# First eight column blocks as whole float32 products, and one pair of places for all operands, in a two-layer hybrid mixer on one Trainium2 core

## The chip, the core and the metric

The kernel runs on one core of a Trainium2 chip. The core has a matmul engine (PE, with a weight-load row PEld beside it), a vector engine (DVE), a scalar engine (ACT), GpSimd (POOL) and SyncE (SP), which here only issues loads. The metric is the device time of one execution in microseconds (us); lower is better.

## What is computed

Two layers over 256 tokens of width 2048. Each layer modulates its normed input by a projection of a condition vector `c`, runs two mixers side by side (a gated linear attention and an RWKV-7 recurrence), projects out, and runs a squared-ReLU feed-forward part:

```python
cond = silu(c)
for i in range(2):
    mod = cond @ w_ada[i] + b_ada[i]                 # 6 x 2048 numbers
    sh1, sc1, gt1, sh2, sc2, gt2 = split(mod, 6)
    h = rmsnorm(x, g_pre_mix[i]) * (1.0 + sc1) + sh1
    z = h @ w_in[i]
    y = concat([gla(z), rwkv7(z)]) @ w_out[i]
    x = x + gt1 * rmsnorm(y, g_post_mix[i])
    h = rmsnorm(x, g_pre_ffn[i]) * (1.0 + sc2) + sh2
    y = square(relu(h @ w_ff1[i])) @ w_ff2[i]
    x = x + gt2 * rmsnorm(y, g_post_ffn[i])
```

Everything is float32.

## The kernel before

**Tiling.** Activations lie transposed: width in 16 slices (index k) of 128 partitions, 256 tokens along the free axis. A *block* is 128 columns of a weight matrix times all 16 slices. Float32 weights are split (`split`): ScalarE copies half a weight tile, 128x1024, to a rounded `hi`, VectorE subtracts to get `lo`. The activations are split the same way into `hh` and `hl`. A block is then 16 times three products: hi·hh, hi·hl, lo·hh, 48 matmuls of 128x256 in all.

**The first stage** is `first_norm`. The norm of layer 0 needs the modulation, so for each k it runs two modulation jobs (`ada_job`, shift row k and scale row 16 + k). A job loads 1 MB of `w_ada` and reduces it against `cond` (which stands in all 128 partitions) in one VectorE instruction, `raw<-raw,cond`; small instructions (`ada_done`) add the bias and form the scale. Then `norm_block` makes slice k: VectorE multiplies x by the norm's `rstd` into `f` (tile name `f512`, two buffers), ScalarE applies scale and shift in place and copies to `hh`, VectorE subtracts to `hl`. Since every block needs all 16 slices, the kernel keeps eight blocks of `w_in` open in eight PSUM banks and grows all eight by slice k as soon as it is there (`grow`): the half megabyte of weights `w8[k]` is split and 8 x 3 matmuls run. Thirty-two modulation loads share six buffers, the sixteen `w8` loads three.

**After it** the first eight blocks are taken out of PSUM (`lerp`, tiles `th`, `gl`, `al`, `o`), and the other blocks of `w_in` run, mixed with the chains of the two mixers. The other modulation jobs are spread over later stages as a background stream.

**Places.** The operands `hh` and `hl` of a stage lie in two buffers of 16 x 256 floats with 64 floats of room; `HOME` gives, for each of six operands, at how many floats from the 256-byte-aligned start `hh` and `hl` begin. Operand 0 is the input of layer 0's mixers, 1 its out projection, 2 its feed-forward input, 3 to 5 the same in layer 1. The squared hidden activations (`hid`) have one pair, 12 and 284, which is 12 and 28 past a multiple of 64.

**Order.** Each engine runs its instructions strictly in the order in which the built program has them. That order is made by a scheduler when the kernel is built, not by the order of the source lines; priorities (`high_priority`) shift it.

Of the kernel before, what the change touches and what calls it, by code (L numbers as in the profile page):

```python
# [8 lines left out]
F32 = mybir.dt.float32  # L9
# [3 lines left out]
ALU = mybir.AluOpType  # L13
# [28 lines left out]
for _name, _n in (("g1", 16), ("gg1", 16), ("g2", 16), ("gg2", 16), ("omu", 29), ("h_k_k", 8), ("h_w0", 8),  # L42
                  ("h_a0", 8), ("h_v0", 8), ("h_k_a", 8), ("c_k_a", 8), ("h_norm_w", 8), ("h_gn_w", 8)):
    _DER[_name] = (NDER, _n)
    NDER += _n
# [50 lines left out]
HOME = ((24, 8), (12, 28), (4, 36), (8, 40), (36, 4), (60, 28))  # L96
# [72 lines left out]
class Kernel:  # L169
# [16 lines left out]
    def setup(self, pool):  # L186
        nc, a, c = self.nc, self.a, self.const

        c1, sg = (pool.tile([P, 512], F32, name=n, bufs=1) for n in ("c1", "sg"))
        nc.gpsimd.memset(c1, 0.0)  # L190
        nc.sync.dma_start(out=c1[0:P:32], in_=a["c"])
        cs = c.tile([P, 4, P], F32, name="cs")
        nc.sync.dma_start(out=cs, in_=a["cst"])
        self.ident, self.bd, self.ones, self.center = (cs[:, n] for n in range(4))
# [4 lines left out]
        self.mod = c.tile([P, 2, 96], F32, name="mod")  # L199
        self.der = c.tile([P, 2, NDER], F32, name="der")  # L200

        self.tanh(sg, c1, scale=0.5)
        nc.vector.scalar_tensor_tensor(c1, sg, 1.0, c1, ALU.add, ALU.mult)
        self.cond = c.tile([P, D], F32, name="cond")
# [7 lines left out]
        self.eps = c.tile([P, 4], F32, name="eps")  # L212
        for n, e in enumerate((1e-6, GN_EPS, KK_SCALE * 1e-24, -KK_SCALE * 1e-24)):
            nc.vector.memset(self.eps[:, n:n + 1], e)
        self.rstd = c.tile([P, T], F32, name="rstd")
        self.shift = c.tile([P, NF], F32, name="shift")
        self.shs = c.tile([P, KT, 2, 2], F32R, name="shs")
        self.vfirst = self.dram.tile([8, P, T], F32, name="vfirst")
        self.spill = self.dram.tile([2, 8, P, 5, T], F32, name="spill")
        self.vmix = self.dram.tile([8, P, T], F32, name="vmix")  # L220

    def constants(self):
        nc = self.nc
        for i in range(2):
# [22 lines left out]

    def tanh(self, out, in_, bias=0.0, scale=1.0, more=()):

        ins = self.nc.scalar.activation(out, in_, AF.Tanh, bias=bias, scale=scale)  # L250
        for o, x, b, c in more:
            ins = self.nc.scalar.activation(o, x, AF.Tanh, bias=b, scale=c)
        with self.tc.issue_after(ins.ins):
            self.nc.scalar.preload_act_table_set(BASE_SET)


    def ada_job(self, i, j, single=None):
# [3 lines left out]
        nc.sync.dma_start(out=raw, in_=self.a["ada"][i, j])  # L261
        nc.vector.tensor_tensor_reduce(  # L262
            out=raw, in0=raw, in1=self.cond, op0=ALU.mult, op1=ALU.add, scale=1.0, scalar=0.0,
            accum_out=self.mod[:, i, j:j + 1])
# [5 lines left out]
    def ada_done(self, i, j0, j1):  # L270

        nc = self.nc
        seg, k = j0 // 16, slice(j0 % 16, j0 % 16 + j1 - j0)
        m = self.mod[:, i, j0:j1]
        nc.vector.tensor_tensor(m, m, self.col(i, "b_ada")[:, j0:j1], op=ALU.add)

        name, g = (None, ("g1", "g_pre_mix"), ("gg1", "g_post_mix"),
                   None, ("g2", "g_pre_ffn"), ("gg2", "g_post_ffn"))[seg] or (None, None)
        if name is None:
            return  # L280
        d = self.dcol(i, name)[:, k]
        if seg in (1, 4):
            nc.vector.scalar_tensor_tensor(d, m, 1.0, self.col(i, g)[:, k], ALU.add, ALU.mult)
        else:
            nc.vector.tensor_tensor(d, m, self.col(i, g)[:, k], op=ALU.mult)
        nc.vector.tensor_scalar(d, d, -0.5 / D, None, ALU.mult)
# [88 lines left out]
    def first_norm(self, pool, rstd):  # L375

        nc = self.nc
# [5 lines left out]
        for k in range(KT):  # L383
            self.ada_job(0, k, pool)
            self.ada_job(0, 16 + k, pool)
            self.norm_block(pool, 0, rstd, 0, k, 1)
# [4 lines left out]
            hi, lo = self.split(raw, P)  # L391
            self.grow(hi, lo, self.hh[:, k], self.hl[:, k], k)

    def boundary(self, pool, i, y, acc, which, ni, src, out=None):
# [27 lines left out]
        for k in range(0, KT, 2):  # L422
            us = []
            self.update(i, y, r, which, k)
            for q in range(2):
# [3 lines left out]
                nc.scalar.activation(u[0][:, :T], self.x[:, k + q], AF.Copy, scale=self.dcol(ni, g, k + q))  # L429
                nc.vector.scalar_tensor_tensor(u[1][:, :T], self.x[:, k + q], self.dcol(ni, g, k + q),  # L430
# [22 lines left out]
    def norm_block(self, pool, i, rstd, which, k, n):  # L453
        nc = self.nc
        g, s0 = ("g1", 0) if which == 0 else ("g2", 48)
        t = pool.tile([P, n, T], F32, name="f512")
        nc.vector.tensor_tensor(t, self.x[:, k:k + n], rstd.unsqueeze(1).broadcast_to([P, n, T]), op=ALU.mult)
        for q in range(n):
            nc.scalar.activation(t[:, q], t[:, q], AF.Identity, scale=self.dcol(i, g, k + q),
                                 bias=self.mod[:, i, s0 + k + q:s0 + k + q + 1])  # L460
        hh, hl = self.hh[:, k:k + n], self.hl[:, k:k + n]
        nc.scalar.copy(hh, t)
        nc.vector.tensor_tensor(hl, t, hh.bitcast(F32), op=ALU.subtract)

# [578 lines left out]
    def layer(self, i):  # L1043
        nc, a = self.nc, self.a
        with ExitStack() as ctx:
# [12 lines left out]
            for m in range(KT):  # L1058
                ps = self.block(a["wout"][i, m], lambda k: oh[:, k], lambda k: ol[:, k], OUT_ORDER)
                nc.scalar.activation(y[:, m], ps, AF.Copy, scale=self.dcol(i, "gg1", m))  # L1060
# [13 lines left out]
            for c in range(4):  # L1074
# [19 lines left out]
                for m in range(KT):  # L1094
# [5 lines left out]
                    if c == 3:  # L1100
                        acc = self.accumulate(pool, acc, y[:, m], m == KT - 1)
                        nc.scalar.activation(y[:, m], y[:, m], AF.Copy, scale=self.dcol(i, "gg2", m))
# [88 lines left out]
def _pack(x):  # L1191
# [4 lines left out]
    a["c"] = f["c"].reshape(4, 512)  # L1196
# [60 lines left out]
```

## Time and profile before

| | us |
|---|---|
| median of 3 runs | 2750.57 (2744.34 to 2753.77) |
| the profiled execution | 2763.49 |
| its span, first to last instruction | 2761.7 |
| busy: PE / PEld | 2624.6 (95%) / 2516.8 (91%) |
| busy: DVE / ACT / POOL | 1994.7 (72%) / 1417.7 (51%) / 67.7 (2%) |
| chain that ended last | PE 76%, DVE 10%, DMA 8%, ACT 3%, issue 2% |

A line number such as L306 is a line of the kernel before. Busy times are sums of durations; matmuls are pipelined, so the time from one matmul's start to the next one's is read instead of the duration. The row PEclk gives the granted clock of PE as a share of 2.4 GHz; it has two levels, 2.4 and 1.2 GHz. The span is one execution; the runs' median lies 12.9 us under the profiled execution's own time.

### The profile page before, as it was taken

To read this page: it belongs to the slowest core of one execution; us is meant where nothing else is said; L and a number is where in the kernel's file an instruction comes from. 1 tells how busy PE (TensorE), PEld (TensorE's weight loads), DVE (VectorE), ACT (ScalarE), POOL (GpSimd) and SP (SyncE) were. 2 spreads that over 40 slices of the span, in tenths; PEclk is the share of its full clock that TensorE was granted. 3 is DMA by queue.
4 is the path that set the end of the run, shared out by engine and by line. 5 is a ranking of instruction groups with operands and counts; after the bars stand their busy time and mean duration, and the time that the engine had idled before them with its cause. 6 is when DMAs were issued, how large, how long until landed. Compare 5 with 4: busy or idle time off the path is not lost.

```text
span 2761.7 us, 55614 instructions
## 1 busy us (share of the span) xinstructions
PE 2624.6 (95%) x23388; PEld 2516.8 (91%) x23388; DVE 1994.7 (72%) x2961; ACT 1417.7 (51%) x2357; POOL 67.7 (2%) x201
## 2 busy tenths in 40 slices
PE   4688999998999999999999999999989999999997
PEld 4688888888999999999989889888989999999997
DVE  8997886678876777777777698666786565565655
ACT  3377644454744534434568866445474443443453
POOL 0000000010000000000001000000000000000000
PEclk8799999999999999999999999999999999999999
DMA  9775576667677877877846547654846666666653
GB/s 402 314 271 187 178 282 238 214 248 274 221 287 285 298 289 277 297 291 281 292 181 224 184 163 254 237 174 163 330 164 216 222 219 214 216 220 220 215 185 120
DMA packets 104082, 659.20 MB, mean 239 GB/s; under 512 B 11540, under 2 KB 20884, under 8 KB 32408
## 3 DMA queue, kind: packets, MB, share of 16 engines
q1 hardware_dynamic: 87848, 618.19, 62.4%
q10 hardware_dynamic: 15984, 37.46, 3.7%
q8 instruction: 183, 3.00, 0.4%
q14 instruction: 67, 0.55, 0.1%
HBM read 638.83 MB, written 16.78 MB: 237 GB/s over the span
## 4 chain that ended last, share of the span: by engine, by line
PE 76%; DVE 10%; DMA 8%; ACT 3%; issue 2%; ACTq 0%; POOL 0%; DVEq 0%; SPq 0%
PE pm L317 13%; PE pm L319 13%; PE pm L318 12%; PE px L319 7%; PE px L317 7%; PE px L318 7%; DMA raw<-in_ada_dram 4%; DVE raw L262 3%; DVE lo L306 3%; PE p L523 1%; DMA raw<-in_ff_dram 1%; ACT hi L305 1%; DMA raw<-in_wout_dram 1%; PE px L470 1%; PE pm L1012 1%
## 5 line engine op out<-in xcount | busy, mean ns | idle before, releaser
L306 DVE TENSOR_TENSOR lo<-raw,hi 128x1024 fp32r<-128x1024 f32 (+1 forms) x792 | 957.4, 1215 | 494.6 <-ACT hi L305 489.6
L305 ACT CAST hi<-raw 128x1024 fp32r<-128x1024 f32 (+1 forms) x792 | 818.7, 1041 | 736.6 <-PE pm L318 305.9
L317 PE MATMUL pm<-hh,hi 128*128 128x256 f32 x2624 | 758.3, 289 | 5.0 <-ACT hi L305 2.7
L319 PE MATMUL pm<-hh,lo 128*128 128x256 f32 x2624 | 745.4, 284 | 5.8 <-DVE lo L306 5.6
L318 PE MATMUL pm<-hl,hi 128*128 128x256 f32 x2624 | 741.3, 283 | 0.0
L317 PEld LDWEIGHTS pm<-hh,hi 128*128 128x128 f32 x2624 | 497.3, 190 | 15.8 <-ACT hi L305 3.3
L319 PEld LDWEIGHTS pm<-hh,lo 128*128 128x128 f32 x2624 | 497.5, 190 | 10.9 <-DVE lo L306 7.3
L318 PEld LDWEIGHTS pm<-hl,hi 128*128 128x128 f32 x2624 | 497.4, 190 | 4.5 <-issue 1.6
L262 DVE CUSTOM_DVE_ANT_0 raw<-raw,cond 128x2048 f32<-128x2048 f32 x192 | 439.2, 2288 | 76.3 <-DMA raw<-in_ada_dram 75.8
L317 PE MATMUL px<-hid,hi 128*128 128x256 f32 x1024 | 287.0, 280 | 0.5 <-ACT hid L1090 0.5
L319 PE MATMUL pm<-hid,lo 128*128 128x256 f32 x1024 | 287.4, 281 | 0.0
L319 PE MATMUL px<-hid,lo 128*128 128x256 f32 x1024 | 287.4, 281 | 0.0
L317 PE MATMUL pm<-hid,hi 128*128 128x256 f32 x1024 | 286.9, 280 | 0.0
L318 PE MATMUL px<-hid,hi 128*128 128x256 f32 x1024 | 285.2, 279 | 0.4 <-DVE hid L1091 0.4
L318 PE MATMUL pm<-hid,hi 128*128 128x256 f32 x1024 | 284.7, 278 | 0.0
L319 PE MATMUL px<-hh,lo 128*128 128x256 f32 x896 | 251.3, 280 | 0.0
L317 PE MATMUL px<-hh,hi 128*128 128x256 f32 x896 | 251.2, 280 | 0.0
L318 PE MATMUL px<-hl,hi 128*128 128x256 f32 x896 | 249.8, 279 | 0.0
L318 PEld LDWEIGHTS px<-hid,hi 128*128 128x128 f32 x1024 | 192.2, 188 | 1.0 <-DVE hid L1091 0.8
L317 PEld LDWEIGHTS px<-hid,hi 128*128 128x128 f32 x1024 | 192.4, 188 | 0.7 <-ACT hid L1090 0.7
L319 PEld LDWEIGHTS px<-hid,lo 128*128 128x128 f32 x1024 | 192.8, 188 | 0.0
L319 PEld LDWEIGHTS pm<-hid,lo 128*128 128x128 f32 x1024 | 192.8, 188 | 0.0
(333 smaller groups left out, 4168.2 us busy)
## 6 DMA issues: line engine op xcount, KB each, us to landing
raw<-in_ff_dram SPq DMA_DIRECT2D x242, 1024.0 KB, 5.0
raw<-in_ada_dram SPq DMA_DIRECT2D x192, 1024.0 KB, 6.3
raw<-in_win_dram SPq DMA_DIRECT2D x90, 1024.0 KB, 5.2
raw<-in_wout_dram SPq DMA_DIRECT2D x32, 1024.0 KB, 5.6
raw<-in_ff1s_dram SPq DMA_DIRECT2D x16, 896.0 KB, 4.7
spill<-pk ACTq DMA_DIRECT2D x16, 640.0 KB, 4.7
pk<-spill ACTq DMA_DIRECT2D x16, 640.0 KB, 5.3
raw<-in_w_dram SPq DMA_DIRECT2D x16, 512.0 KB, 10.4
```

Source lines behind the costliest of these rows:

```text
L262: nc.vector.tensor_tensor_reduce(out=raw, in0=raw, in1=self.cond, op0=ALU.mult, op1=ALU.add, scale=1.0, scalar=0.0, accum_out=self.mod[:, ...
L305: self.nc.scalar.copy(hi, half)
L306: self.nc.vector.tensor_tensor(lo, half, hi.bitcast(F32), op=ALU.subtract)
L317: nc.tensor.matmul(ps, hi[:, n % 8], xh(k), start=n == 0, stop=False)
L318: nc.tensor.matmul(ps, hi[:, n % 8], xl(k), start=False, stop=False)
L319: nc.tensor.matmul(ps, lo[:, n % 8], xh(k), start=False, stop=n == KT - 1)
L470: self.nc.tensor.matmul(ps, self.ones, sq[:, q], start=k + q == 0, stop=k + q == KT - 1)
L523: self.nc.tensor.matmul(v[:, h, n + c], l[hs, cs], r[hs, cs], start=True, stop=True)
L1012: nc.tensor.matmul(vps[c], hh[:, kk, cs], hi[:, kq], start=kk == 0, stop=False)
```

## The change

- The first eight blocks are no longer split. `first_norm` multiplies the float32 tile `w8[k]` with the float32 tile `f` (returned by `norm_block`), one matmul for each block and slice; 384 matmuls of split operands become 128 of whole float32, and 16 `hi` copies on ScalarE and 16 `lo` subtractions on VectorE go. `hh` and `hl` are still made, for the later blocks.
- `ada_done` goes. Two tables, `factor` and `start`, are made once for each layer (`ada_tables`), and a job multiplies by its factor within its reduction; shift rows take `start` in there too, the others get one addition. Scales are read from `mod` (`mcol`), no longer from `der`.
- `c` is broadcast to all partitions by its load (1 MB written). The sigmoid then runs on the full 128x2048 in two halves; the four matmuls and four copies that spread `cond` go. The loads of x and of the constants change queues: x goes from ScalarE's queue to SP's, ahead of the modulation loads.
- All six operands lie at 12 and 28.

```diff
-HOME = ((24, 8), (12, 28), (4, 36), (8, 40), (36, 4), (60, 28))
+HOME = ((12, 28),) * 6
@@ setup
-        nc.sync.dma_start(out=c1[0:P:32], in_=a["c"])
+        nc.sync.dma_start(out=self.cond, in_=a["c"].broadcast_to([P, D]))
         for k in range(0, KT, 4):
-            nc.scalar.dma_start(out=self.x[:, k:k + 4], in_=a["xT"][:, k:k + 4])
+            nc.sync.dma_start(out=self.x[:, k:k + 4], in_=a["xT"][:, k:k + 4])
-        for n in range(0, D, 512):
-            ps = self.psm.tile([P, 512], F32, name="pm")
-            r = slice(n // 16, n // 16 + 1)
-            nc.tensor.matmul(ps, self.ones[r], c1[r], start=True, stop=True)
-            nc.scalar.activation(self.cond[:, n:n + 512], ps, AF.Copy, scale=0.5)
+            for h in halves:
+                nc.vector.scalar_tensor_tensor(self.cond[:, h], sg[:, h], 1.0, self.cond[:, h], ALU.add, ALU.mult)
+            self.ada_tables(0)
@@ ada_job
         nc.vector.tensor_tensor_reduce(
-            out=raw, in0=raw, in1=self.cond, op0=ALU.mult, op1=ALU.add, scale=1.0, scalar=0.0,
-            accum_out=self.mod[:, i, j:j + 1])
-        if single:
-            self.ada_done(i, j, j + 1)
-        elif j % 16 == 15:
-            self.ada_done(i, j - 15, j + 1)
+            out=raw, in0=raw, in1=self.cond, op0=ALU.mult, op1=ALU.add, scale=self.factor[:, i, j:j + 1],
+            scalar=self.start[:, i, j:j + 1] if small else 0.0, accum_out=self.mod[:, i, j:j + 1])
+        if not small and (single or j % 16 == 15):
+            js = slice(j if single else j - 15, j + 1)
+            nc.vector.tensor_tensor(self.mod[:, i, js], self.mod[:, i, js], self.start[:, i, js], op=ALU.add)
@@ first_norm
-            self.norm_block(pool, 0, rstd, 0, k, 1)
+            h = self.norm_block(pool, 0, rstd, 0, k, 1)
@@
-            hi, lo = self.split(raw, P)
-            self.grow(hi, lo, self.hh[:, k], self.hl[:, k], k)
+            w = raw.rearrange("p (n c) -> p n c", c=P)
+            for n, (ps, _, _) in enumerate(self.first):
+                nc.tensor.matmul(ps, w[:, n], h[:, 0], start=k == 0, stop=k == KT - 1)
```

The change also moves instructions. On VectorE, one k step late in the first stage stood so before (`raw` are modulation tiles, `f512` the normed slice before the split, ISA the reduction and the read of its sum; a name in brackets is the engine whose work is waited for):

```order
L262 ISA raw_743,mod_97<-raw_743,cond_102 128x2048 [waits DMAHW7_49]
L262 ISA mod_97 128x1
L275 TENSOR_TENSOR mod_97<-mod_97,par_91 128x1 [waits DVE_49]
L262 ISA raw_747,mod_97<-raw_747,cond_102 128x2048 [waits DMAHW0_49]
L262 ISA mod_97 128x1
L275 TENSOR_TENSOR mod_97<-mod_97,par_91 128x1 [waits DVE_49]
L283 SCALAR_TENSOR_TENSOR der_98<-mod_97,par_91 128x1 [waits DVE_49]
L286 TENSOR_SCALAR der_98<-der_98 128x1 [waits DVE_49]
L306 TENSOR_TENSOR lo_761<-raw8_758,hi_760 128x1024 [waits DMAHW1_49,PE_49,Activation_49]
L463 TENSOR_TENSOR hl_150<-f512_753,hh_149 128x256 [waits Activation_49]
L457 TENSOR_TENSOR f512_865<-x_84,rs_142 128x256 [waits DVE_49]
```

Between the scale (L286), which ScalarE waits for, and `hl`, which waits for ScalarE, stands the 128x1024 subtraction. On VectorE after the change, two k steps early in the first stage:

```order
L284 ISA raw_202,mod_101<-raw_202,cond_86,start_103,factor_102 128x2048 [waits DMAHW6_49]
L462 TENSOR_TENSOR f512_231<-x_84,rs_142 128x256 [waits DVE_49,PE_49]
L284 ISA raw_205,mod_101<-raw_205,cond_86,factor_102 128x2048 [waits DMAHW7_49]
L289 TENSOR_TENSOR mod_101<-mod_101,start_103 128x1 [waits DVE_49]
L468 TENSOR_TENSOR hl_150<-f512_209,hh_149 128x256 [waits Activation_49]
L284 ISA raw_224,mod_101<-raw_224,cond_86,start_103,factor_102 128x2048 [waits DMAHW1_49]
L284 ISA raw_227,mod_101<-raw_227,cond_86,factor_102 128x2048 [waits DMAHW2_49]
L462 TENSOR_TENSOR f512_253<-x_84,rs_142 128x256 [waits DMAHW5_49,DVE_49,PE_49]
L289 TENSOR_TENSOR mod_101<-mod_101,start_103 128x1 [waits DVE_49]
L468 TENSOR_TENSOR hl_150<-f512_231,hh_149 128x256 [waits Activation_49]
```

(The reads of the sums are left out.) `hl` now stands directly behind the addition that releases ScalarE, and `f`, whose buffer is read by the matmuls of two slices earlier, waits for PE; it stands alternately between the two reductions and behind both. At the end of the first stage VectorE has after the change (`lo` here is of the first block after the stage, `th` the first block taken out of PSUM):

```order
L468 TENSOR_TENSOR hl_150<-f512_473,hh_149 128x256 [waits Activation_49]
L309 TENSOR_TENSOR lo_595<-raw_592,hi_594 128x1024 [waits DMAHW5_49,Activation_49]
L309 TENSOR_TENSOR lo_599<-raw_592,hi_598 128x1024 [waits Activation_49]
L284 ISA raw_518,mod_101<-raw_518,cond_86,start_103,factor_102 128x2048 [waits DMAHW6_49]
L284 ISA raw_521,mod_101<-raw_521,cond_86,factor_102 128x2048 [waits DMAHW7_49]
L289 TENSOR_TENSOR mod_101<-mod_101,start_103 128x1 [waits DVE_49]
L468 TENSOR_TENSOR hl_150<-f512_525,hh_149 128x256 [waits Activation_49]
L284 ISA raw_715,mod_101<-raw_715,cond_86,factor_102 128x2048 [waits DMAHW1_49]
L309 TENSOR_TENSOR lo_721<-raw_718,hi_720 128x1024 [waits DMAHW2_49,Activation_49]
L514 SCALAR_TENSOR_TENSOR th_568<-pm_152,par_93,th_568 128x255 [waits DMAHW4_49,DMAHW0_49,Activation_49]
```

Before, the first two of these `lo` stood behind the last `hl`, and the third reduction and the third `lo` behind `th`. After the first stage the scheduler places many instructions of layer 0's mixers in another order; the feed-forward parts keep theirs.

## Rows read from the trace of the kernel before

**Rows 1.** Stretches: us; busy (count) of PE, PEld, DVE, ACT, POOL; PEclk, DMA, GB/s.

```profile
20.00:64.00 44.00, 24.43 (x144) 23.19 (x144) 44.00 (x77) 12.31 (x19) 0.00 (x0) 0.88 1.02 418
64.00:129.00 65.00, 40.36 (x222) 38.14 (x223) 63.19 (x102) 18.60 (x29) 0.12 (x1) 0.76 0.86 344
```

**Rows 2.** Timeline of one k step: start, duration, engine, line, operation, count.

```profile
114.82 0.42 DVE L457 TENSOR_TENSOR f<-x,rs 128x256 f32<-128x256 f32 x1
...
115.16 2.28 DVE L262 CUSTOM_DVE_ANT_0 raw<-raw,cond 128x2048 f32<-128x2048 f32 x1
...
117.57 2.29 DVE L262 CUSTOM_DVE_ANT_0 raw<-raw,cond 128x2048 f32<-128x2048 f32 x1
...
119.90 0.16 DVE L275 TENSOR_TENSOR mod<-mod,par 128x1 f32<-128x1 f32 x1
...
120.28 0.15 DVE L286 TENSOR_SCALAR der<-der 128x1 f32<-128x1 f32 x1
120.39 1.22 DVE L306 TENSOR_TENSOR lo<-raw,hi 128x1024 fp32r<-128x1024 f32 x1
120.47 0.60 ACT L459 ACTIVATE f<-f,mod,der 128x256 f32<-128x256 f32 x1 [5.19 <-DVE der L286]
...
121.54 0.42 DVE L463 TENSOR_TENSOR hl<-f,hh 128x256 fp32r<-128x256 f32 x1
...
121.89 2.28 DVE L262 CUSTOM_DVE_ANT_0 raw<-raw,cond 128x2048 f32<-128x2048 f32 x1
```

**Rows 3.** Timeline: first reduction with what precedes it; second and sixteenth `hl`.

```profile
13.71 1.05 ACT L1136 ACTIVATE sq<-x 128x1024 f32<-128x1024 f32 x1
...
16.06 0.69 DVE L1139 TENSOR_TENSOR acc<-acc 128x512 f32<-128x512 f32 x1
...
18.86 2.28 DVE L262 CUSTOM_DVE_ANT_0 raw<-raw,cond 128x2048 f32<-128x2048 f32 x1
...
33.27 0.42 DVE L463 TENSOR_TENSOR hl<-f,hh 128x256 fp32r<-128x256 f32 x1
...
128.26 0.42 DVE L463 TENSOR_TENSOR hl<-f,hh 128x256 fp32r<-128x256 f32 x1
```

**Rows 4.** Timeline behind the first stage: split, first blocks' exit, next block's first matmul.

```profile
130.23 2.36 DVE L306 TENSOR_TENSOR lo<-raw,hi 128x1024 fp32r<-128x1024 f32 x2 [1.54 <-ACT hi L305]
...
132.51 0.48 DVE L508 SCALAR_TENSOR_TENSOR th<-pm,par,th 128x255 f32<-128x255 f32 x1
...
133.03 0.38 PE L317 MATMUL pm<-hh,hi 128*128 128x256 f32 x1 [0.33 <-DVE th L508]
```

**Rows 5.** Timeline, float32 matmuls, two records each: at 1.2 GHz, at 2.4 GHz.

```profile
16.80 2.07 PE L347 MATMUL px<-acc,cs 128*128 128x256 f32 x4 [0.86 <-DVE acc L1139]
...
579.24 1.03 PE L803 MATMUL px<-gl,wsmB 128*128 128x256 f32 x4
```

**Rows 6.** One line's instructions: ns least, median, most; first and last start.

```profile
L347 PE MATMUL px<-acc,cs x12: 377/378/793, 16.8 to 2744.8; 128*128 128x256 f32 x12
```

**Rows 7.** Timeline of split matmuls in one k step, 1.2 GHz.

```profile
123.53 0.41 PE L373 MATMUL px<-hh,lo 128*128 128x256 f32 x1
123.74 0.41 PE L371 MATMUL px<-hh,hi 128*128 128x256 f32 x1
```

**Rows 8.** Timeline, first matmuls of blocks 15 blocks apart: layer 1, then layer 0.

```profile
2203.55 0.28 PE L317 MATMUL px<-hh,hi 128*128 128x256 f32 x1
...
2288.34 0.28 PE L317 MATMUL pm<-hh,hi 128*128 128x256 f32 x1
...
2299.64 0.28 PE L317 MATMUL pm<-hid,hi 128*128 128x256 f32 x1
...
2383.91 0.28 PE L317 MATMUL px<-hh,hi 128*128 128x256 f32 x1
...
1050.08 0.28 PE L317 MATMUL px<-hh,hi 128*128 128x256 f32 x1
...
1133.29 0.28 PE L317 MATMUL pm<-hh,hi 128*128 128x256 f32 x1
```

More of the change, by code (lines that the diff above doesn't have):

```diff
@@ L41 @@
 NDER = 0
-for _name, _n in (("g1", 16), ("gg1", 16), ("g2", 16), ("gg2", 16), ("omu", 29), ("h_k_k", 8), ("h_w0", 8),
+for _name, _n in (("omu", 29), ("h_k_k", 8), ("h_w0", 8),
                   ("h_a0", 8), ("h_v0", 8), ("h_k_a", 8), ("c_k_a", 8), ("h_norm_w", 8), ("h_gn_w", 8)):
@@ L187, in setup @@
         nc, a, c = self.nc, self.a, self.const
-        c1, sg = (pool.tile([P, 512], F32, name=n, bufs=1) for n in ("c1", "sg"))
-        nc.gpsimd.memset(c1, 0.0)
-        nc.sync.dma_start(out=c1[0:P:32], in_=a["c"])
-        cs = c.tile([P, 4, P], F32, name="cs")
-        nc.sync.dma_start(out=cs, in_=a["cst"])
-        self.ident, self.bd, self.ones, self.center = (cs[:, n] for n in range(4))
+        sg = pool.tile([P, D], F32, name="sg", bufs=1)
+        self.cond = c.tile([P, D], F32, name="cond")
+        self.eps = c.tile([P, 4], F32, name="eps")
+        for n, e in enumerate((1e-6, GN_EPS, KK_SCALE * 1e-24, -KK_SCALE * 1e-24)):
+            nc.vector.memset(self.eps[:, n:n + 1], e)
+        nc.sync.dma_start(out=self.cond, in_=a["c"].broadcast_to([P, D]))
         self.par = c.tile([P, 2, NPAR], F32, name="par")
@@ L197, in setup @@
         for k in range(0, KT, 4):
-            nc.scalar.dma_start(out=self.x[:, k:k + 4], in_=a["xT"][:, k:k + 4])
-        self.mod = c.tile([P, 2, 96], F32, name="mod")
-        self.der = c.tile([P, 2, NDER], F32, name="der")
-        self.tanh(sg, c1, scale=0.5)
-        nc.vector.scalar_tensor_tensor(c1, sg, 1.0, c1, ALU.add, ALU.mult)
-        self.cond = c.tile([P, D], F32, name="cond")
-        for n in range(0, D, 512):
-            ps = self.psm.tile([P, 512], F32, name="pm")
-            r = slice(n // 16, n // 16 + 1)
-            nc.tensor.matmul(ps, self.ones[r], c1[r], start=True, stop=True)
-            nc.scalar.activation(self.cond[:, n:n + 512], ps, AF.Copy, scale=0.5)
+            nc.sync.dma_start(out=self.x[:, k:k + 4], in_=a["xT"][:, k:k + 4])
+        cs = c.tile([P, 4, P], F32, name="cs")
+        nc.scalar.dma_start(out=cs, in_=a["cst"])
+        self.ident, self.bd, self.ones, self.center = (cs[:, n] for n in range(4))
+        self.mod, self.factor, self.start = (c.tile([P, 2, 96], F32, name=n) for n in ("mod", "factor", "start"))
+        self.der = c.tile([P, 2, NDER], F32, name="der")
+        with self.tc.high_priority(1000):
+            early = pool.tile([P, 1], F32, name="early", bufs=1)
+            ins = nc.scalar.activation(early, self.eps[:, 0:1], AF.Tanh)
+            with self.tc.issue_after(ins.ins):
+                halves = [slice(n, n + D // 2) for n in (0, D // 2)]
+                self.tanh(sg[:, halves[0]], self.cond[:, halves[0]], scale=0.5,
+                          more=[(sg[:, halves[1]], self.cond[:, halves[1]], 0.0, 0.5)])
+            for h in halves:
+                nc.vector.scalar_tensor_tensor(self.cond[:, h], sg[:, h], 1.0, self.cond[:, h], ALU.add, ALU.mult)
+            self.ada_tables(0)
         self.xres = self.dram.tile([P, KT, T], F32, name="xres")
-        self.eps = c.tile([P, 4], F32, name="eps")
-        for n, e in enumerate((1e-6, GN_EPS, KK_SCALE * 1e-24, -KK_SCALE * 1e-24)):
-            nc.vector.memset(self.eps[:, n:n + 1], e)
         self.rstd = c.tile([P, T], F32, name="rstd")
@@ L223, in constants @@
         nc = self.nc
+        self.ada_tables(1)
         for i in range(2):
@@ L246, in dcol, with mcol @@
         return self.der[:, i, at + k:at + k + 1]
+    def mcol(self, i, name, k):
+        j = 16 * ("s1", "g1", "gg1", "s2", "g2", "gg2").index(name) + k
+        return self.mod[:, i, j:j + 1]
     def tanh(self, out, in_, bias=0.0, scale=1.0, more=()):
@@ L254, in tanh, with ada_tables @@
             self.nc.scalar.preload_act_table_set(BASE_SET)
+    def ada_tables(self, i):
+        nc = self.nc
+        f, s, b = self.factor[:, i], self.start[:, i], self.col(i, "b_ada")
+        nc.vector.memset(f, 0.5)
+        for seg, g in ((1, "g_pre_mix"), (2, "g_post_mix"), (4, "g_pre_ffn"), (5, "g_post_ffn")):
+            nc.vector.tensor_scalar(f[:, 16 * seg:16 * seg + 16], self.col(i, g), -0.25 / D, None, ALU.mult)
+        nc.vector.scalar_tensor_tensor(s, b, 2.0, f, ALU.mult, ALU.mult)
+        for seg in (1, 4):
+            q = slice(16 * seg, 16 * seg + 16)
+            nc.vector.scalar_tensor_tensor(s[:, q], f[:, q], 2.0, s[:, q], ALU.mult, ALU.add)
     def ada_job(self, i, j, single=None):
@@ L454, in norm_block @@
         nc = self.nc
-        g, s0 = ("g1", 0) if which == 0 else ("g2", 48)
+        g, s = ("g1", "s1") if which == 0 else ("g2", "s2")
         t = pool.tile([P, n, T], F32, name="f512")
```

31 lines of the change are left out of this document (9 added, 22 removed).

## The prediction

> **What bounds the kernel now.** I read the busy time by stretches first. Over most of the span PE is full and VectorE is not; the exception is the first stage, up to 129 us, where PE is busy little more than half the time and VectorE nearly all of it (44.00 of 44, then 63.19 of 65) [rows 1]. Loads stand close behind: 418 GB/s with all DMA engines busy in the earlier stretch, 344 in the later [rows 1]. So the first stage ends when VectorE is through with its 16 steps, and the change is aimed there. The timeline of one step shows its length: its first reduction starts at 115.16, that of the next at 121.89, 6.73 us, and the `f` multiply, which this step happens to lack, adds 0.34: 7.1 [rows 2]. Over the whole stage, from the second `hl` at 33.27 to the sixteenth at 128.26, 14 steps take 94.99 us, 6.79 each; the early ones are shorter [rows 3]. Behind the stage the exit `th` starts at 132.51 and the next block's first matmul, which waits for it, at 133.03 [rows 4]. After that, the second thing to read is the pace of PE: the time from one matmul's start to the next, by operand.
>
> **A step after the change, on VectorE.** By the new order a step holds two reductions, one `f`, one addition and one `hl`. First reduction 2.28; second 2.33 to the addition (117.57 to 119.90); `f` 0.34 (114.82 to 115.16); from the instruction that releases ScalarE to `hl` 1.26 (120.28 to 121.54: ScalarE's norm starts 0.19 on, then its copy to `hh`); `hl` to the next reduction 0.35 (121.54 to 121.89) [rows 2]. Sum 6.56 us. The `lo` of 1.22, which filled that 1.26 before, is gone, but the 1.26 stays, now as idle time, because `hl` stands directly behind the addition. The removal of `lo` is therefore worth almost nothing; what goes is the three small instructions and their gaps. The 16 `hi` copies lay beside other work on ScalarE, which waited 5.19 us for VectorE in that step [rows 2]: worth nothing.
>
> **PE and the new wait.** A float32 matmul of 128x256 is two records. Four records take 1.03 us at 2.4 GHz and 2.07 at 1.2 GHz; the last lasts 0.38 and 0.79 [rows 5, 6], so a record starts every (1.03 - 0.38)/3 = 0.217 us, or (2.07 - 0.79)/3 = 0.427. Eight matmuls are 16 records: 15 x 0.217 + 0.38 = 3.63 us, or 15 x 0.427 + 0.79 = 7.20. Before, 24 split matmuls took 24 x 0.117 = 2.8 us at the pace of [rows 8], or 24 x 0.21 = 5.0 at the low level [rows 7]. They were hidden either way. Now `f` has two buffers and PE reads it, so VectorE waits at `f` for the products of the slice two before, with everything queued behind: the reductions, hence the release of load buffers, and the addition that lets the next product start. PE starts 0.19 + 0.60 + 0.03 = 0.82 us after the addition. Where `f` stands between the reductions VectorE gets there 1.26 + 0.35 + 2.28 = 3.89 after it, elsewhere 6.17. At 2.4 GHz PE ends at 0.82 + 3.63 = 4.45: waits of 0.56 and 0, mean 0.28, a step of 6.84. At 1.2 GHz it ends at 8.02: waits 4.13 and 1.85, mean 2.99, a step of 9.55. The granted clock was 0.76 of full in the late steps and 0.88 in the early ones [rows 1], with 2.8 us of full-speed work in 7.1; now 3.6 stand in about 7, so I take a fifth of the records at the low level, under the half that 0.76 would mean: 12 x 0.217 + 3 x 0.427 + 0.38 = 4.27, waits of 1.20 and 0, a step of 7.16.
>
> **The stage.** Start: the four matmuls and copies that spread `cond` go, and no `lo` stands between the fold at 16.06 + 0.69 = 16.75 and the first reduction, which was at 18.86 [rows 3]. c and x now go ahead of the modulation loads on SP's queue: 3.1 MB at 418 GB/s, 7.5 us, while before x shared the engines with them. The squares need all of x, as they did. I take 2 us earlier; bounds 0 and 3. Steps: 14 x (7.16 - 6.79) = 5.2 later. Two `lo` of the next block, 2.36 [rows 4], now stand ahead of the last pair of reductions. The last `hl` is then at 128.26 - 2 + 5.2 + 2.4 = 133.9, PE's last product ends at 133.9 - 1.26 + 0.82 + 4.27 = 137.7, and `th`, which now has a reduction and a third `lo` ahead of it (2.28 + 1.15), starts at 137.7 too. The next block starts 4.7 us later than at 133.03 [rows 4]. But 2.28 + 1.15 = 3.4 of VectorE's later work is then done, and VectorE is wanted there. So the stage costs between 1.3 and 4.7; I take 3. The other jobs of the kernel's modulation lose a few small instructions that PE's work hides: nothing. The scheduler's other order in layer 0's mixers I cannot price: one reduction of 2.3 put on the path or taken off it, so 2.3 either way, taken at 0.
>
> **The places.** Fifteen blocks are 720 matmuls. In layer 1's feed-forward part `hh` and `hl` at (60, 28) take 2288.34 - 2203.55 = 84.79 us, 117.8 ns each; `hid`, at the pair that all operands get, 2383.91 - 2299.64 = 84.27, 117.0 [rows 8]. That is 0.7 ns, with the same weights buffers; the addresses of these move by a whole 1024 bytes. In layer 0's third quarter, at (4, 36), blocks run at 83.21/720 = 115.6 [rows 8]. So the pace hangs on more than places. At 0.7 ns: 57 blocks of layer 1's feed-forward part 57 x 48 x 0.7 = 1.9 us; 41 blocks of layer 0's at the slower pace 1.4 (taken as layer 1's), 16 at the quick one -1.1; 16 of the out projection 0.5; some 90 blocks of the mixers 3.0, of which I count half, since they wait for more than PE. Sum 4.2; I take 4. Bounds: 0 (places are not what sets it) and 10 (the 57 + 41 feed-forward blocks at 115.6: 98 x 48 x 2.2 ns).
>
> **The sum.** The profiled execution took 2763.5; 2763.5 + 3 - 4 = 2762.5. The median of the runs lies 12.9 under it: 2749.6, so **2750 us**, no change that can be measured. About 0.3%, 8.3 us, is what can be told from none.
>
> **Rivals.**
> *Loads become the bound.* If VectorE did not idle at `hl` and `f`, a step would be as long as its loads: 2.62 MB at 418 GB/s, 6.27 us [rows 1]. Then 14 x (6.27 - 6.79) = -7.3; the last `hl` falls to 121.3, PE ends at 121.3 - 0.44 + 3.63 = 124.5, 8.5 before 133.03; with the places, and a part of the 3.4 of work done early, 13: 2737.5. For it: VectorE's busy time a step is only some 5.7 (two reductions, `f`, `hl` and an addition, 2 x 2.28 + 2 x 0.42 + 0.16, [rows 2]). Against it: the new order. The Trainium skill ("DMA: Bandwidth & Descriptors", "Where 436 GB/s comes from") puts loads from HBM at some 358 GB/s for a core; by that the loads of a step would take 7.3 us and there would be nothing to gain here. The trace shows 418 over 44 us, and that decides.
> *The low clock holds.* Every wait at `f` leaves PE idle until addition and norm are through. If the products run mostly at 1.2 GHz, VectorE and PE wait for each other in turn. With two thirds of the records low a product takes 5.7 us, the waits are 2.7 and 0.4, a step 8.1: 14 x (8.1 - 7.16) = 13 more, 2763; with all low, 2783. It decides from a mean step of 7.8, which is 9 us over mine. For it: the 0.76 of [rows 1]. Against it: more work in a step. By the Trainium skill ("TensorE: Matmul & The Clock Gate", "HAM oscillation — how this bites in real kernels") work in bursts between waits can fall to half clock in each pause and then starts every burst there; by that alone this rival would be the likeliest, 2783 at its worst. The early stretch, at 0.88 with the same kind of bursts, speaks for less.
> *The places do nothing*, the pace being set elsewhere: 2763.5 + 3 - 12.9 = 2753.6, still no measurable change.
>
> **How the numbers follow.** Forecast 0.47, places inert 0.15, loads bound 0.20, low clock 0.18. Faster by over 0.3%: the loads' case and a tail of the forecast, 0.25; slower: the clock's case, 0.18; within: 0.57. The range goes from the loads' case, 2737, to the lower end of the clock's, 2764.
>
> **What would show it.** In the changed profile: steps of about 7.1 between `hl`s; VectorE idle some 1.1 us before each `hl` with ScalarE's copy as releaser, and before every other `f` with PE as releaser; the next block's first matmul near 138; blocks of `hh` at 117.0 ns in layer 1's feed-forward part. Steps near 6.3 with reductions waiting for loads, or steps over 7.8, would prove me wrong, as would blocks still at 117.8.

## The result and the profile after

The changed kernel takes 2778.8 us (median of 6) beside 2753.3 for the kernel before: ratio 1.0095, 95% interval 1.007 to 1.012. A second series gave 1.0099 (1.0077 to 1.0121). It is slower by some 26 us; the forecast was no change that can be measured, 2750 us, with a range from 2737 to 2764. Its profiled execution has a span of 2785.6 us beside 2761.7.

The first stage comes first. Stretches of the changed kernel, with the columns of [rows 1]:

```profile
20.00:64.00 44.00, 28.70 (x96) 22.18 (x96) 34.29 (x46) 6.87 (x15) 0.00 (x0) 0.92 1.02 419
64.00:129.00 65.00, 41.71 (x139) 32.49 (x140) 50.11 (x64) 10.93 (x20) 0.00 (x0) 0.84 0.89 359
```

VectorE (third busy time) was full before; now it idles for a fifth of the time, and the stage still grows. The timeline of VectorE, two steps (start, duration, engine, line, operation; in brackets idle time and what ended it), beside [rows 2]:

```profile
111.35 0.42 DVE L468 TENSOR_TENSOR hl<-f,hh 128x256 fp32r<-128x256 f32 x1 [1.16 <-ACT hh L467]
111.70 2.40 DVE L284 CUSTOM_DVE_ANT_0 raw<-raw,cond,start 128x2048 f32<-128x2048 f32 x1
...
114.03 2.35 DVE L284 CUSTOM_DVE_ANT_0 raw<-raw,cond,factor 128x2048 f32<-128x2048 f32 x1
...
116.38 0.42 DVE L462 TENSOR_TENSOR f<-x,rs 128x256 f32<-128x256 f32 x1
116.72 0.15 DVE L289 TENSOR_TENSOR mod<-mod,start 128x1 f32<-128x1 f32 x1
118.04 0.42 DVE L468 TENSOR_TENSOR hl<-f,hh 128x256 fp32r<-128x256 f32 x1 [1.17 <-ACT hh L467]
...
121.39 0.42 DVE L462 TENSOR_TENSOR f<-x,rs 128x256 f32<-128x256 f32 x1 [0.59 <-PE p L397]
121.73 2.35 DVE L284 CUSTOM_DVE_ANT_0 raw<-raw,cond,factor 128x2048 f32<-128x2048 f32 x1
...
125.44 0.42 DVE L468 TENSOR_TENSOR hl<-f,hh 128x256 fp32r<-128x256 f32 x1 [1.16 <-ACT hh L467]
```

From the second `hl` on, steps of some 6.69 and 7.40 us alternate, but for one of 8.05 and a last one of 9.58 with two `lo` in it: `hl` waits 1.16 us for ScalarE in each, `f` some 0.59 for PE in every other. Waits of VectorE between 20 and 140 us of the changed kernel (us in all, times, longest):

```profile
DVE hl L468 <- ACT hh L467: 18.5, 16, 1.5
DVE f L462 <- PE p L397: 6.8, 9, 1.4
```

And the end of the stage, beside [rows 4] (timeline of PE, ScalarE, VectorE):

```profile
134.60 1.75 PE L397 MATMUL pm<-f,raw 128*128 128x256 f32 x6 [4.17 <-ACT f L464]
136.14 2.76 PE L397 MATMUL px<-f,raw 128*128 128x256 f32 x6
...
140.04 0.47 ACT L513 ACTIVATE th<-pm,der 128x256 f32<-128x256 f32 x1 [4.12 <-PE p L397]
...
140.55 0.48 DVE L514 SCALAR_TENSOR_TENSOR th<-pm,par,th 128x255 f32<-128x255 f32 x1 [1.70 <-ACT th L513]
...
141.09 0.39 PE L320 MATMUL pm<-hh,hi 128*128 128x256 f32 x1 [1.08 <-DVE th L514]
```

The next block starts at 141.09 instead of 133.03: 8.1 us, a third of the loss. The rest is found by comparing the same marks in both traces: A is the first matmul of the sum behind layer 0's out projection (`px<-acc`), B the same behind its feed-forward part. The table has every profiled kernel; the experiments are told below. *Fold* stands for factor and start taken into the reduction.

| kernel | next block at | A | B | A to B | ratio to before |
|---|---|---|---|---|---|
| before | 133.0 | 671.7 | 1410.4 | 738.7 | 1 |
| before, again (e5) | 133.0 | 667.9 | 1408.2 | 740.3 | 1 |
| changed | 141.1 | 678.6 | 1426.2 | 747.6 | 1.0095 |
| changed, again (e6) | 140.8 | 677.9 | 1429.2 | 751.3 | 1.0099 |
| e1 no fold | 145.3 | 674.2 | 1416.5 | 742.3 | 1.0047 |
| e2 old places | 140.2 | 676.0 | 1424.0 | 748.0 | 1.0096 |
| e3 split products | 131.3 | 668.5 | 1410.5 | 742.0 | 1.0013 |
| e4 before + whole products | 145.0 | 674.2 | 1422.7 | 748.5 | 1.0038 |
| e7 four f buffers | 139.6 | 677.1 | 1424.8 | 747.7 | 1.0102 |
| e8 + late hl, no fold | 139.0 | 669.9 | 1410.8 | 740.9 | 1.0035 |
| e9 fold in stage only | 142.9 | 679.5 | 1420.6 | 741.1 | 1.0050 |
| e10 ordered stage | 127.7 | 668.6 | 1418.4 | 749.8 | 1.0017 |
| e11 ordered, fold in stage only | 127.0 | 662.9 | 1408.1 | 745.2 | 0.9995 |
| e12 split, fold in stage only | 131.0 | 664.2 | 1402.5 | 738.3 | 0.9999 |
| e13 ordered, no fold | 127.3 | 663.1 | 1407.8 | 744.7 | 0.9996 |
| e14 no fold in that part | 140.8 | 682.5 | 1422.1 | 739.6 | 1.0069 |

A comes 7 to 10 us later, about as the next block does. Then 9 to 11 us more are lost between A and B, in layer 0's feed-forward part. There the changed reduction shows. Groups of VectorE's instructions in that part (count | busy us, mean ns | idle before, releaser), the changed kernel:

```profile
L284 DVE CUSTOM_DVE_ANT_0 raw<-raw,cond,factor 128x2048 f32<-128x2048 f32 x47 | 110.5, 2350 | 35.8 <-DMA raw<-in_ada_dram 35.5
L284 DVE CUSTOM_DVE_ANT_0 raw<-raw,cond,start 128x2048 f32<-128x2048 f32 x16 | 38.6, 2411 | 22.0 <-DMA raw<-in_ada_dram 22.0
```

and the kernel before:

```profile
L262 DVE CUSTOM_DVE_ANT_0 raw<-raw,cond 128x2048 f32<-128x2048 f32 x63 | 144.3, 2290 | 54.1 <-DMA raw<-in_ada_dram 53.7
```

With the factor read per partition a reduction takes 0.06 us longer, with the start too 0.12. That is 47 x 0.06 + 16 x 0.12 = 4.7 us in this part. The idle times suggest why it isn't hidden: VectorE waits for the load in front of 50 of the 63, and SP, which issues the loads in their order, waits for a `lo` of VectorE to free the buffer before 35 of these loads, 40.0 us in all (before: 34, 40.0). So VectorE and the loads wait for each other in a ring. That the ring passes the added time on is a reading; no run isolates it. The reduction in front of the last `hid` of the third quarter (timeline of VectorE, ScalarE, PE in the changed kernel):

```profile
1152.52 2.35 DVE L284 CUSTOM_DVE_ANT_0 raw<-raw,cond,factor 128x2048 f32<-128x2048 f32 x1 [1.09 <-DMA raw<-in_ada_dram]
...
1154.80 0.42 DVE L1094 TENSOR_TENSOR sq<-rl 128x256 f32<-128x256 f32 x1
...
1155.25 0.41 ACT L1096 CAST hid<-sq 128x256 fp32r<-128x256 f32 x1 [3.85 <-DVE sq L1094]
...
1155.71 0.38 PE L320 MATMUL px<-hid,hi 128*128 128x256 f32 x1 [2.14 <-ACT hid L1096]
```

The same reduction before, then in e4, where reductions have constant factors as before:

```profile
1140.12 2.29 DVE L262 CUSTOM_DVE_ANT_0 raw<-raw,cond 128x2048 f32<-128x2048 f32 x1 [0.33 <-DMA raw<-in_ada_dram]
```

```profile
1151.67 2.29 DVE L262 CUSTOM_DVE_ANT_0 raw<-raw,cond 128x2048 f32<-128x2048 f32 x1 [1.80 <-DMA raw<-in_ada_dram]
```

What is late at this place is the load: VectorE waits 0.33 us for it before, 1.09 in the changed kernel and 1.80 in e4.

PE's waits for `hid` between 779 and 1411 us (us in all, times, longest): changed kernel, then its second profile, then before:

```profile
PE px L320 <- ACT hid L1096: 4.0, 3, 2.1
```

```profile
PE px L320 <- ACT hid L1096: 5.1, 3, 2.7
```

```profile
PE px L317 <- ACT hid L1090: 0.5, 1, 0.5
```

Behind the longer ones the granted clock falls. Stretches of PE with the third and the fourth quarter's wait (us; busy, count; clock, DMA, GB/s), where nearly all others have 32.00 busy and 1.00:

```profile
1138.00:1170.00 32.00, 29.20 (x235) 0.95 0.81 284
1330.00:1362.00 32.00, 30.41 (x244) 0.95 0.81 293
```

Behind B the profiles differ mainly by how long the low clock lasted in layer 1's mixers, and that changes from one execution to the next: from B to the sum behind layer 1's out projection the two profiles of the changed kernel show 604 and 597 us. No single one is read there. Taken together they do differ: 589 to 604 (mean 599) in the seven profiles with the fold in those mixers, 586 to 594 (mean 590) in the nine without. Part of that is chance, since a profiled execution lay up to some 16 us off its kernel's median.

Where the change was meant to help PE, it did: blocks of `hh` in layer 1's feed-forward part, the counterpart of [rows 8], 720 matmuls apart:

```profile
2229.16 0.28 PE L320 MATMUL px<-hh,hi 128*128 128x256 f32 x1
...
2313.43 0.28 PE L320 MATMUL pm<-hh,hi 128*128 128x256 f32 x1
```

84.27 us, 117.0 ns each, where it was 84.79.

### The profile page after: what moved, and what is told of

Its sections match the earlier page's. It is cut to its first block, busy times and chain, and to the rows that moved or that the text cites. A ratio compares the mean times of both kernels' runs of the same rounds, so it can differ in the third digit from the quotient of the medians.

```text
span 2785.6 us, 55263 instructions
## 1 busy us (share of the span) xinstructions
PE 2639.2 (95%) x23252; PEld 2516.7 (90%) x23252; DVE 1987.3 (71%) x2897; ACT 1401.3 (50%) x2341; POOL 67.9 (2%) x200
## 4 chain that ended last, share of the span: by engine, by line
PE 67%; DMA 11%; DVE 8%; ACT 3%; issue 2%; ACTq 0%; POOL 0%; DVEq 0%; SPq 0%
PE pm L320 11%; PE pm L322 11%; PE pm L321 11%; DMA raw<-in_ada_dram 9%; PE px L320 6%; PE px L322 6%; PE px L321 6%; DVE raw L284 2%; DVE lo L309 2%; DMA raw<-in_wout_dram 1%; PE p L529 1%; ACT hi L308 1%; PE pm L1018 1%; PE pm L1019 1%; PE pm L1020 1%
## 5 line engine op out<-in xcount | busy, mean ns | idle before, releaser
L309 DVE TENSOR_TENSOR lo<-raw,hi 128x1024 fp32r<-128x1024 f32 (+1 forms) x776 | 936.9, 1215 | 490.4 <-ACT hi L308 486.3
L308 ACT CAST hi<-raw 128x1024 fp32r<-128x1024 f32 (+1 forms) x776 | 797.2, 1041 | 721.0 <-PE pm L321 278.0
L284 DVE CUSTOM_DVE_ANT_0 raw<-raw,cond,factor 128x2048 f32<-128x2048 f32 x128 | 300.5, 2347 | 49.1 <-DMA raw<-in_ada_dram 48.6
L320 PEld LDWEIGHTS pm<-hid,hi 128*128 128x128 f32 x1024 | 193.7, 189 | 0.0
```

The costliest lines, as they stand in the source:

```text
L284: nc.vector.tensor_tensor_reduce(out=raw, in0=raw, in1=self.cond, op0=ALU.mult, op1=ALU.add, scale=self.factor[:, i, j:j + 1], scalar=self ...
L308: self.nc.scalar.copy(hi, half)
L309: self.nc.vector.tensor_tensor(lo, half, hi.bitcast(F32), op=ALU.subtract)
L320: nc.tensor.matmul(ps, hi[:, n % 8], xh(k), start=n == 0, stop=False)
```

## The experiments

Three theories. **S**: the loss is the first stage's new waits. **R**: it is the longer reduction, added up where VectorE has no slack. **P**: it is the places. In the code, `...` stands for what is left out.

**e1, no fold.** The reductions as before, factor and start put on afterwards:

```diff
-            out=raw, ..., scale=self.factor[:, i, j:j + 1],
-            scalar=self.start[:, i, j:j + 1] if small else 0.0, ...
+            out=raw, ..., scale=1.0, scalar=0.0, ...
+            nc.vector.tensor_tensor(m, m, self.factor[:, i, js], op=ALU.mult)
+            nc.vector.tensor_tensor(m, m, self.start[:, i, js], op=ALU.add)
```

> The changed kernel with one part undone: the modulation reductions run with constant factors (1.0 and 0.0) as before, and the factor and the start are put on the result by two small VectorE instructions, per column in the first stage and per 16 columns later. Theory R (the reduction with a factor per partition takes 2.35 to 2.41 us where it took 2.29; in layer 0's feed-forward part each reduction waits for a load that waits for a buffer which VectorE frees behind the reduction before, so the 0.06 to 0.12 us of 63 reductions add up until PE waits for hid): reductions back at 2.29, layer 0's feed-forward part (first to last hid block) back from 640.5 to about 631.5 us, the whole 9 to 16 us under the changed kernel, 2763 to 2770 beside 2753 for the kernel before. Theory S (all of the loss comes from the first stage): stage within 1 us of the changed kernel's, whole unchanged at about 2778. Theory P (the loss comes from the places of the operands): unchanged, 2778.

Measured 1.0047 (1.0029 to 1.0065), 2768.6 us. Reductions are back at 2.29 us and the whole falls as R said, although the first stage got longer (145.3; the two small instructions stand in each step). A to B fell by 5 to 9 us, to 742.3, where R said 9. S alone falls.

**e2, old places.** `HOME` of the kernel before.

> The changed kernel with the operands at the six pairs of places of the kernel before. Theory P (the common places cost time in layer 0's feed-forward part and in layer 1's mixers): 2758 to 2765 beside 2753 before, with no PE waits for hid in layer 0's feed-forward part. Theories R and S: the loss stays and the 2 us gained in layer 1's feed-forward part go: blocks of hh there at 117.8 ns instead of 117.0, whole 2779 to 2784; feed-forward part of layer 0 still about 640 us.

1.0096 (1.0063 to 1.0128): the loss stays. P falls. The pace of `hh` blocks returned to 117.8 ns, but what the places give lies inside the interval.

**e3, split products.** In `first_norm`:

```diff
-            w = raw.rearrange("p (n c) -> p n c", c=P)
-            for n, (ps, _, _) in enumerate(self.first):
-                nc.tensor.matmul(ps, w[:, n], h[:, 0], start=k == 0, stop=k == KT - 1)
+            hi, lo = self.split(raw, P)
+            self.grow(hi, lo, self.hh[:, k], self.hl[:, k], k)
```

> The changed kernel with the first eight blocks as split products again (hi, lo, hh, hl), all else as changed. Theory S: the next block's first matmul falls from 141.1 to 133 to 136 us, and the whole by 5 to 8 to about 2771 beside 2753 before. Theory R: the first stage gives back the same 5 to 8, layer 0's feed-forward part keeps its 640 us. If the whole falls by 15 or more, the later stages follow the first stage's order and not the reduction.

1.0013 (0.9994 to 1.0032). The next block starts 9.8 us earlier, at 131.3; `lo` fills the time in which `hl` waited, and nearly every step is 6.79. The whole fell by 23, more than the stage gave, which was the sign named for later stages that follow the first stage and not the reduction; A to B fell to 742 with the longer reductions in place. Here R fails.

**e4, whole products alone**, the reverse of e3's edit on the kernel before.

> The kernel before with one part of the change alone: whole float32 products in the first stage. Theory S: next block's first matmul at 138 to 141 instead of 133, whole 5 to 8 us over the kernel before, 2758 to 2761 beside 2753; if all of the change's loss is the products', 2778. Theory R: reductions at 2.29, layer 0's feed-forward part at about 631 us as before, whole 2756 to 2761.

1.0038 (1.0022 to 1.0054), 2766.9. The stage lost 11.9 us (next block at 145.0), more than S said, and the whole 10 to 12. A to B took 748.5 with reductions at 2.29, and in that part VectorE and PE run their instructions in exactly the order of the kernel before: neither the length of the reduction nor its order explains this one.

**e5, the kernel before once more, and e6, the changed kernel once more.**

> The kernel before, unchanged, profiled a second time, to see which of its stage lengths repeat. Expected to repeat within 1 us by every theory: the next block's first matmul at 133.0, the first ones sum of the out projection of layer 0 at 671.7. Open: layer 0's feed-forward part with its boundary, 738.7 us in the first profile, while four variants took 742 to 748.5; theory R (longer reductions) expects 739 again, a theory of chance in the loads of that part expects 742 to 748. Layer 1's mixers are expected to differ with the time at the low granted clock, by half of it.

> The changed kernel, unchanged, profiled a second time and timed in more rounds. Expected: ratio 1.008 to 1.010, next block's first matmul at 141.1, layer 0's out projection reached at 678 to 679; layer 0's feed-forward part 747.6 again if its waits belong to the kernel, 739 to 742 if they were chance.

The first stage repeats within 0.3 us, A within 4 (not within the 1 us expected), A to B within 2 and 4. The waits in layer 0's feed-forward part belong to the changed kernel.

**e7, four buffers for `f`** (`bufs=4`; the norm's `rs` two instead of four).

> The changed kernel with four buffers for the first stage's f instead of two, so that VectorE no longer waits for PE there (the room comes from two unused buffers of the norm). Theory S (the stage's new waits are the loss, and the stage is passed on to the end): steps between hl's 6.7 us each instead of 6.7 and 7.4 in turn, no idle time of VectorE with PE as releaser in the stage, next block's first matmul at 135 to 137 instead of 141.1, whole 4 to 6 us under the changed kernel. Theory R: the whole stays within 3 us of the changed kernel, since the later waits stay.

1.0102 (1.0075 to 1.0129), next block at 139.6: no gain. Waits of VectorE, 20 to 139 us:

```profile
DVE f L462 <- PE p L397: 5.9, 8, 1.3
```

The wait is nearly as long as with two (6.8). The scheduler puts an `f` as far ahead as there are buffers, so with four it asks for the buffer that PE is reading just then. More buffers don't remove a wait that the order makes.

**e8, also `hl` later, no fold** (`hl` of a slice queued behind the next slice's first reduction; e1's reductions).

> The changed kernel with three edits: four buffers for f, each slice's hl put behind the next slice's first reduction (so that VectorE no longer idles for ScalarE's norm and copy), and the reductions with constant factors, factor and start put on by two small instructions. Theory S: steps as long as their loads, 6.3 us (5.8 is VectorE's own sum), next block's first matmul at 124 to 128, 17 to 21 us before that of the changed kernel with plain reductions (145.3); if the stage is passed on, the whole at 2748 to 2753 beside 2755 before, ratio 0.998 to 1.000. If the mixers give the stage's time back, as they gave back 9 of the 12 us that this stage cost with plain reductions, ratio 1.001 to 1.004.

1.0035 (1.002 to 1.005), next block at 139.0. The waits at `hl` are gone, but those at `f` grew from 6 to 19 us: one wait took the place of the other. The expected 124 to 128 was missed, since `f` again stands as far ahead as there are buffers.

**e9, fold in the first stage only**: the changed kernel with `scale=self.factor[...] if single else 1.0`, and e1's two small instructions elsewhere.

> The changed kernel with the factor and the start folded into the reduction in the first stage only; the other 160 reductions run with constant factors and are scaled and shifted per 16 columns. Theory R (the longer reduction, and the other order that the scheduler makes of it, cost 8 us in layer 0's mixers, 5 in its feed-forward part, 4 in layer 1's mixers): next block's first matmul at 141 as in the changed kernel, layer 0's mixers with out projection back from 537 to 529 us, its feed-forward part from 748 to 751 back to 739 to 743, the whole at ratio 1.003 to 1.005 instead of 1.0097. If the first stage alone were the cause, ratio 1.009 to 1.010.

1.0050 (1.003 to 1.007). Against 1.0095 and 1.0099 the fold behind the stage costs some 13 us, give or take 8 by the intervals, with the stage as slow as ever (142.9). A to B is 741.1. Layer 0's mixers did not go back to 529 us (142.9 to 679.5 is 536.7): that part of R was wrong. The fold also makes the scheduler order the mixers and that part otherwise: VectorE's order differs from before at 15 places in layer 0's feed-forward part and at some 20 in layer 1's mixers with the fold, at none and at most one without. The section on the change says that the feed-forward parts keep their order; in layer 0's, VectorE's did not. How much is duration and how much order these runs don't separate.

**e10, ordered stage**: two buffers, `f` and the `hl` of the slice before queued behind the slice's first reduction.

```diff
+            with self.tc.issue_after(ins.ins):          # ins: the slice's first reduction
+                nc.vector.tensor_tensor(t[:, 0], self.x[:, k], rstd, op=ALU.mult)
+                nc.vector.tensor_tensor(self.hl[:, k - 1], prev[:, 0], self.hh[:, k - 1].bitcast(F32), ...)
```

> The changed kernel with two instructions of each step put in another place of VectorE's order, with the same two buffers: a slice's f, and the hl of the slice before, stand behind the slice's first reduction. Then f finds its buffer free (the product of two slices before ended a step earlier) and hl finds ScalarE done. Theory S for the stage: no wait of VectorE for PE or ScalarE in the steps, which are then as long as their loads, 6.3 us (VectorE's own sum is 5.5), next block's first matmul at 124 to 128 instead of 141. Theory R: the later stages keep their loss of 14 to 17 us, so the whole falls by what the stage gives, to 1.004 to 1.006; if instead the later loss came from the late start of the mixers, the whole falls by 20 us or more, to 1.000 to 1.002.

1.0017 (0.9997 to 1.0038), next block at 127.7. VectorE's timeline, one step, and its waits between 25 and 139 us:

```profile
85.81 2.41 DVE L284 CUSTOM_DVE_ANT_0 raw<-raw,cond,start 128x2048 f32<-128x2048 f32 x1 [0.69 <-DMA raw<-in_ada_dram]
...
88.14 0.42 DVE L466 TENSOR_TENSOR f<-x,rs 128x256 f32<-128x256 f32 x1
88.48 0.42 DVE L468 TENSOR_TENSOR hl<-f,hh 128x256 fp32r<-128x256 f32 x1
88.82 2.35 DVE L284 CUSTOM_DVE_ANT_0 raw<-raw,cond,factor 128x2048 f32<-128x2048 f32 x1
...
92.08 2.41 DVE L284 CUSTOM_DVE_ANT_0 raw<-raw,cond,start 128x2048 f32<-128x2048 f32 x1 [0.71 <-DMA raw<-in_ada_dram]
```

```profile
DVE raw L284 <- DMA raw<-in_ada_dram: 9.4, 13, 1.1
```

Now the loads bound the stage: 6.25 us a step, against the 6.27 that the prediction worked out for this rival. The whole fell by some 22 us, 13 of them the stage's. As in e3, that is the sign named for a later loss that comes from the first stage, and not R's; A to B is no guide here (749.8), for the profiled execution, at 2774, lay 16 us above the median.

**e11, both edits; e12, split products with the fold in the stage only.**

> Both edits together: f and hl behind the first reduction, and the fold in the first stage only. If the stage's and the reduction's share add up: next block's first matmul at 124 to 128, layer 0's mixers at 529 to 535 us, its feed-forward part at 739 to 743, the whole 0.996 to 1.000 of the kernel before (2742 to 2753). If the stage's gain is given back in the mixers, 1.001 to 1.004.

> The changed kernel with split products again and the fold in the first stage only: what is left of the change is the load of c, the fold in the first stage and the places. Theory R: next block's first matmul at 131.3 as in the run with split products, feed-forward part of layer 0 at 739 to 741 instead of 742, layer 1's mixers some 4 us shorter than there, the whole 0.998 to 1.000 of the kernel before. If the longer reductions cost nothing behind split products, 1.001 as there.

0.9995 (0.9976 to 1.0014) and 0.9999 (0.9982 to 1.0015): both level with the kernel before, so the stage and the fold behind it hold the loss between them, as far as the intervals tell. In e11 A to B stayed at 745.2, over the 739 to 743 expected. From e9 to e11 the stage's 15.9 us came through whole (15). From e10 to e11 the fold behind the stage costs 6 us, from e3 to e12 some 4, inside the intervals, beside 13 from the changed kernel to e9: by these medians its price is high only behind the slow first stage.

**e13, ordered stage, no fold anywhere.**

> The changed kernel with f and hl behind the first reduction and no fold anywhere: constant factors in all reductions, factor and start put on by two small instructions. VectorE's own sum of a step is 5.9 us, under the loads' 6.25. If the fold in the stage is what makes layer 0's mixers longer: next block's first matmul at 127 to 129, out projection of layer 0 reached 529 to 531 us later (657 to 660 instead of 662.9), the whole 0.996 to 0.998 of the kernel before. If not, mixers at 535 to 541 as with the fold in the stage, and the whole at 0.999 to 1.001.

0.9996 (0.9975 to 1.0016). Mixers and out projection of layer 0 took 535.8 us, so the fold in the stage isn't what makes them longer. No variant beats the kernel before beyond what can be measured: in e11 and e13 the next block starts 6 us earlier and A is reached 5 to 9 us earlier, and layer 0's feed-forward part takes 5 us of it back, with waits for `hid`.

**e14, no fold in that part alone** (64 reductions).

> The changed kernel with constant factors for the 64 reductions of layer 0's feed-forward part alone, scaled and shifted there per 16 columns; fold kept in the first stage and in the mixers of both layers. If most of the 13 us lie in that part: it takes 739 to 743 us instead of 748 to 751, the whole at 1.005 to 1.007 instead of 1.0097. If they lie in layer 1's mixers, 1.008 to 1.010 with that part at 748.

1.0069 (1.0046 to 1.0092), A to B 739.6 instead of 748 to 751: about 8 of the 13 us lie there, as R expected, though by the ratios alone that is hardly clear of the intervals; what remains to e9's 1.0050 would lie in the mixers of both layers.

## Why the prediction was wrong

**The steps that failed** are two terms of the sum, and that they were added as if each stood alone. The first is one sentence: "The other jobs of the kernel's modulation lose a few small instructions that PE's work hides: nothing." It priced the instructions that go and took the one that stays at its old duration. The reduction went from 2.29 to 2.35 and 2.41 us, and the cover was not there: 54 us of waiting for loads in front of the reductions of layer 0's feed-forward part stood in the trace of before. Measured 13 us (e9), some 8 of them there (e14). The second is the stage, 3 forecast and 8 measured at the next block. And they don't add: undoing the stage alone brings back 22 to 23 us (e10, e3), undoing the fold behind it alone 13 (e9), but both together 27 to 28 (e11, e12). From the other end, whole products alone cost some 10 us (e4) and all the rest of the change some 4 (e3), together 26. So some 7 to 12 us, by the second reckoning beyond the intervals, arise only where both meet, and the sum had no term for that.

**The step on VectorE** was right: 7.16 forecast, 7.17 measured ((125.44 - 32.28) / 13), with 1.16 us idle at `hl` and PE ending the wait at every other `f`. That it came so close is luck: two small errors cancelled. A step without a wait took 6.69 instead of 6.56, since the reductions were longer, and the waits at `f` came to 6.8 us in all instead of 14 x 0.6 = 8.4.

**The stage** was mis-sized: 3 forecast with bounds of 1.3 and 4.7, 8 measured. Its start was right (first reduction at 17.3, 16.9 forecast), and the load of c cost nothing. The last `hl` came at 135.0 instead of 133.9; the last product took 5.4 us (134.60 to 140.0) instead of 4.27, the six records in its middle at half clock (2.76 us; the six before them 1.75); the sum let VectorE's exit follow PE at once, where ScalarE's exit stands between (140.04 to 140.55); and it took the start of `th`, 137.7, for that of the next block, which stands 0.52 behind `th` [rows 4]. Of VectorE's work done early, taken to give 1.7 back, nothing shows at A: 678.6 and 677.9 against 671.7 and 667.9.

**The places**: the pace came out as forecast (117.0), the gain in part. Layer 1's feed-forward part with what follows to its sum took 738.0 and 739.3 us against 739.8 and 740.8; over all profiles, 738.2 with the common places (twelve) and 740.0 with the old (four), where 1.9 was forecast for it. The rest of the 4 us isn't seen, and e2 shows nothing in the whole. The 16 quick blocks of [rows 8] lost their 115.6 ns, as the sum allowed.

**The rivals.** The low clock didn't hold: the mean step, 7.17, stayed under 7.8, and the granted clock in the stage rose, from 0.88 and 0.76 to 0.92 and 0.84. The Trainium skill ("TensorE: Matmul & The Clock Gate", "HAM oscillation — how this bites in real kernels") has such bursts fall to half clock in each pause; the trace shows that in parts of some bursts only: in seven of the sixteen slices the product ran at full clock throughout, in 3.72 us, in the others in 5.3 to 6.8. The loads' rival didn't happen in the changed kernel, but e10 made it happen by order alone, at the step worked out; its gain of 13 us did not come, since even e11 and e13 are only level with the kernel before. The Trainium skill ("DMA: Bandwidth & Descriptors", "Where 436 GB/s comes from") puts loads at some 358 GB/s; e10's stage moved 419, so this trace doesn't agree. The forecast's sum, with the sizes measured in the changed kernel, reads 8 (stage) + 13 (reductions) - 2 (places) = 19 of the 26 us.

**What stays open.** With whole products and plain reductions layer 0's feed-forward part takes 739.6 to 748.5 us (e1, e4, e8, e9, e11, e13, e14), with split ones 738.3 to 740.3 (before twice, e12), though VectorE's order there is the same but for one place in e14. That accounts for about 4 of the missing 7 us; why a different first stage is felt there, and why the fold costs more behind a slow one, wasn't found.

Of the signs named beforehand all came true but one (the next block at 141.1, not near 138), and the time was still wrong: they looked at the stage and the pace, and at no instruction outside.

## What to carry to other kernels

When an instruction takes over the work of others, price what it takes itself, everywhere it runs, before counting what goes away. Two losses that feed the same later stages can cost more together than their sum, so undo each alone and both at once (e3, e9, e12). An engine that idles a third of the time may still have little slack: where it waits for loads, and the loads wait for buffers that it frees, don't take added work as hidden. A wait for a buffer that the scheduler's order makes is removed by order, not by more buffers (e7 against e10).

## What was not expected of the hardware

The same reduction of 128x2048 float32 took 2.29 us with constant factors, 2.35 with a factor per partition, 2.41 with a factor and a start. And small waits of PE can cost twice: in both profiles of the changed kernel two stretches of half clock in layer 0's feed-forward part followed PE's waits of 1.5 to 2.7 us for `hid`. In the kernel before, where PE waited there for at most 1.0 us at a time, none stood between 779 us and the end of that part.
